# Five of the seven small steps of the row scales of x's second half move from VectorE to GpSimd

## The chip, the cores and the metric

The kernel runs on one core of a Trainium2 chip. Such a core has five engines that each work through their own queue of instructions in order: TensorE (PE; its weight loads are listed as PEld), VectorE (DVE), ScalarE (ACT), GpSimd (POOL) and SyncE (SP), which here only issues transfers. They wait for each other by semaphores. The metric is the time of one execution on the device, in microseconds; a kernel's number is the median of its timed runs.

## The reference, cut to what matters

The reference is one layer of a decoder: it normalises its input x (1024 rows of 1024 channels), scales and shifts it with a modulation that depends on c, projects it with w_in and feeds two mixers, whose outputs are merged and projected again. Only the beginning matters here:

```python
def rms_norm(x, g):
    x32 = x.astype(jnp.float32)
    y = x32 * lax.rsqrt(jnp.mean(x32 * x32, axis=-1, keepdims=True) + RMS_EPS)
    return (y * g.astype(jnp.float32)).astype(x.dtype)
...
    mod = jax.nn.silu(c) @ w_mod + b_mod
    shift, scale, gate = jnp.split(mod, 3, axis=-1)
    h = rms_norm(x, norm_g) * (1 + scale[:, None]) + shift[:, None]
    proj = h @ w_in
```

Each row of x has one scale, 1 / sqrt(mean of squares + 1e-6).

## The kernel before

x lies in eight tiles `x_sb` of 128 rows by 1024 channels, in pairs. The function `turn(half)` takes four of these tiles. For each pair, ScalarE squares both tiles and sums each row (line 229, `junk`), so that the first two columns of a small tile `st` of 128x8 hold two sums per partition. `rstd_of` turns them into two scales in seven instructions on 128x2 values: multiply and add (L87), a square root on ScalarE (L88), a reciprocal (L89), and one Newton step on it (L93 to L96), which mends the root. Six of the seven stand on VectorE. Then VectorE multiplies both tiles of the pair by their scales (L232), 128x1024 each. TensorE turns each 128x128 block of the four tiles (L236) into banks `xt`, eight banks of 128x512 for eight blocks of 128 channels, and ScalarE or VectorE copies them out to `xT` (L238; in the second half all copies are ScalarE's). A bank can be filled only when all four tiles of the half are scaled.

Beside this runs `modulation(dt)` for each of eight blocks of channels: VectorE forms `acc` from five eighths of w_mod's block (L251, then four times L253), TensorE adds the other three eighths and `acc` in matrix products of one column (L258, L262, called products here), and VectorE makes the pair `ab` of scale and shift from it (L270, L271). ScalarE then writes h = xT * scale + shift twice (L286 rounded `h_hi`, L287 full `hf`), VectorE their difference `h_lo` (L288), and TensorE multiplies h with three blocks of w_in (L137 to L139, `qi_ps`), 18 matrix products of 128x512 for each block of channels, 144 in all. The first of these for block 0 need only the first half of the rows. The last of the 144 ends at 75.2 us, and the rest of the kernel builds on h.

Nothing of the order on the engines is written by hand here, but for a few `order` calls: the framework builds the program with a scheduler that plans with modelled times, so the order in which an engine's instructions stand follows from what the planner thinks is ready first. The queues are strict: an instruction that waits holds up all that stand behind it on its engine.

`turn(0)` handles tiles 0 to 3, `turn(1)` tiles 4 to 7. In the orders below x_sb_110 is the pair of tiles 4 and 5, x_sb_113 the pair of tiles 6 and 7; st_283 and st_297 hold their scales.

Of the kernel before, what the change touches and what calls it, by code (L numbers as in the profile page):

```python
# [14 lines left out]
OP = mybir.AluOpType  # L15
# [4 lines left out]
D = 1024  # L20
# [5 lines left out]
EPS = 1e-6  # L26
# [8 lines left out]
def tile_hybrid(ctx, tc, x, c, norm_g, w_mod, b_mod, w_in, a_re, a_im, b_re, b_im,  # L35
                c_re, c_im, d_skip, log_dt, w_glu, b_glu, w_a_o, w_b_o, w_out,
                final_g, out):
    nc = tc.nc
# [17 lines left out]
    def bank(name):  # L56
        return ps1.tile([128, 512], F32, name=name, tag="b1")
# [15 lines left out]
    def staged(name, dtype=F32, shape=(128, L)):  # L73
        return stage.tile(list(shape), dtype, name=name, tag="sg")
# [7 lines left out]
        tc.add_manual_dep(later.ins, earlier.ins.name, mybir.DependencyInfo(  # L82
            mybir.DependencyClass.NoSync, mybir.DependencyReason.DATA), reason="order")

    def rstd_of(t, n=1):
        a, b, y, r = (t[:, i * n:(i + 1) * n] for i in range(4))
        nc.vector.tensor_scalar(a, a, 1.0 / D, EPS, op0=OP.mult, op1=OP.add)  # L87
        nc.scalar.sqrt(b, a)  # L88
        nc.vector.reciprocal(y, b)  # L89
        if n == 1:  # L90
            nc.vector.scalar_tensor_tensor(b, y, a, y, op0=OP.mult, op1=OP.mult)
        else:
            nc.vector.tensor_mul(b, y, y)  # L93
            nc.vector.tensor_mul(b, b, a)
        nc.vector.tensor_scalar(b, b, -0.5, 1.5, op0=OP.mult, op1=OP.add)
        nc.vector.tensor_mul(r, y, b)  # L96
        return r
# [75 lines left out]
    with ExitStack() as st:  # L173
# [49 lines left out]
        def turn(half):  # L223

            for t2 in range(4 * half, 4 * half + 4, 2):
                stat = p0.tile([128, 8], F32, name=f"st{t2}", tag="st", bufs=4)
                for t in (t2, t2 + 1):
                    junk = p0.tile([128, D], BF, name=f"junk{t}", tag="junk", bufs=1)
                    nc.scalar.activation(junk, x_sb[t], AF.Square, accum_out=stat[:, t - t2:t - t2 + 1])
                rstd = rstd_of(stat, 2)  # L230
                for t in (t2, t2 + 1):
                    nc.vector.tensor_scalar_mul(x_sb[t], x_sb[t], rstd[:, t - t2:t - t2 + 1])  # L232
            for k in range(ND):
                ps = bank(f"xt{half}_{k}")
                for j in range(4):
                    nc.tensor.transpose(ps[:, 128 * j:128 * j + 128],  # L236
                                        x_sb[4 * half + j][:, 128 * k:128 * k + 128], ident)
                (nc.scalar.copy if k in ((0, 1, 3, 5, 7), (0, 1, 2, 3, 4, 5, 6, 7))[half] else nc.vector.tensor_copy)(  # L238
                    xT[k][:, 512 * half:512 * half + 512], ps)

        turn(0)
        h_hi, h_lo = parts(ND, "h")
        mp = bank("mod_ps")
# [29 lines left out]

        modulation(0)
        turn(1)
        modulation(1)
        qps = [[dense_bank(f"qi{m}_ps") if 2 * m + j < 3 else bank(f"qi{m}_ps") for j in range(2)]
               for m in range(3)]
        for dt in range(ND):
# [5 lines left out]
            for sl in [slice(512 * j, 512 * j + 512) for j in range(2)] if dt < 2 else [slice(0, L)]:  # L285
# [3 lines left out]
                for m in range(3):  # L289
                    a = slice(128 * m, 128 * m + 128)  # L290
                    for j in range(sl.start // 512, sl.stop // 512):
                        b = slice(512 * j, 512 * j + 512)
# [47 lines left out]
    with ExitStack() as st:  # L340
# [23 lines left out]
        for e in range(2):  # L364
            a = slice(64 * e, 64 * e + 64)
# [98 lines left out]
        for i in groups[0] + groups[1]:  # L464
            w = 128 * (i + 1)
            for h in range(8):
                for o, n in chunks(w):
# [5 lines left out]
                    r = p1.tile([128, 512], F32, name=f"r{i}_{h}_{o}", tag="r", bufs=3)  # L473
# [4 lines left out]
                    else:  # L478
                        nc.vector.scalar_tensor_tensor(dst, r[:, :n], wi_t[:, i, h:h + 1], dst,  # L479
                                                       op0=OP.mult, op1=OP.add)  # L480
# [102 lines left out]
    for m in range(4):  # L583
# [3 lines left out]
        for half in range(2):  # L587
# [62 lines left out]
            for ri in range(2):  # L650
# [11 lines left out]
                                         op0=OP.mult, op1=OP.add)  # L662
# [5 lines left out]
            for e in range(2):  # L668
                a = slice(64 * e, 64 * e + 64)
# [25 lines left out]
    t = staged("vraw")  # L695
# [27 lines left out]
    for kt in range(ND):  # L723
        t = staged(f"wg{kt}")
# [5 lines left out]
    b = staged("bgate")[0:1]  # L730
# [30 lines left out]
    def scr(name, dtype=F32, n=6):  # L761
        return sepool.tile([128, n], dtype, name=name)
# [10 lines left out]
    half = scr("half", n=STEPS + 2)  # L773
# [258 lines left out]
    for k, (m, pieces) in enumerate(steps):  # L1032
# [8 lines left out]
        t = wpool.tile([128, D], F32, name=f"wo{k}", tag="wraw")  # L1041
# [7 lines left out]
    for t in range(NT):  # L1049
        tok = slice(128 * t, 128 * t + 128)  # L1050
        xr, y = xy[:, t % 2], xy[:, 2 + t % 2]
        nc.sync.dma_start(xr, x[tok])
        stat = const.tile([128, 8], F32, name=f"fs{t}", tag="fs", bufs=2)
# [12 lines left out]
        if t < NT - 1:  # L1066
            rstd = rstd_of(stat)
            nc.vector.scalar_tensor_tensor(y, y, rstd, fg, op0=OP.mult, op1=OP.mult)
            nc.sync.dma_start(out[tok], y)
        else:  # L1070
            a, b = slice(0, 512), slice(512, 1024)
            nc.gpsimd.tensor_mul(y[:, a], y[:, a], fg[:, a])
            nc.vector.tensor_add(stat[:, 0:1], stat[:, 0:1], stat[:, 6:7])
            rstd = rstd_of(stat)
# [32 lines left out]
```

## Time and profile before

| | us |
|---|---|
| median of 3 runs | 905.14 (904.68 to 906.53) |
| the profiled execution's own time | 904.93 |
| its span, first to last instruction | 903.2 |

TensorE is busy for 95% of the span, VectorE for 73%, ScalarE for 45%, GpSimd for 15%. In the page's 40 slices (22.6 us each) TensorE's first slice stands at 4 tenths, and all others but six at 9. The clock that was granted to TensorE has two levels, 1.2 and 2.4 GHz, which the profile writes as 0.50 and 1.00; its second slice shows 7 tenths. A timeline gives each row as start, duration, engine, line, operation, tiles written <- tiles read, and in brackets how long the engine was idle before it and for whom; rows of equal instructions that follow each other are merged (x2), and an instruction's row may overlap the next one's by its last tenth of a microsecond. TensorE's products show as two rows each.

### The profile page before, as it was taken

Reading aid. Unit: us, or ns where it says so; the run is one execution under the profiler, and the core shown is the slowest. Engines: PE = TensorE matmul, PEld = TensorE weight load, DVE = VectorE, ACT = ScalarE, POOL = GpSimd, SP = SyncE. Lnnn points to the kernel's source line nnn. Section 1 sums busy time; section 2 is a strip of 40 time slices with the busy share of each in tenths; the row PEclk is TensorE's granted clock in tenths of the full one; section 3 lists DMA queues with packets and bytes.
Section 4 is the critical chain, followed back from the end, with each engine's and each line's share of the span. In section 5 each row is a group of like instructions: output and inputs, shape, how many; then the busy total and the mean of one; then the engine's idle time right before and its main releaser. Section 6 shows DMA issues by size and latency. Waiting matters only on the chain. (4 is left out here: it accounts for less than half of the span.)

```text
span 903.2 us, 12003 instructions
## 1 busy us (share of the span) xinstructions
PE 854.9 (95%) x4105; PEld 704.1 (78%) x4105; DVE 655.7 (73%) x1381; ACT 406.5 (45%) x803; POOL 138.4 (15%) x244
## 2 busy tenths in 40 slices
PE   4999999998889998999989999999999999999996
PEld 4887788876678876878868888887888888777885
DVE  5674898488999895588236776678987776856753
ACT  7552576344446443322235555448564443432311
POOL 0000100069455944000000000000000000221000
PEclk9799999999899999999999999999999999999999
DMA  9925611363443423473334232235224232644431
GB/s 330 319 66 126 154 49 46 66 178 91 122 113 124 113 78 99 124 279 94 117 107 128 88 97 73 70 106 166 68 64 135 71 94 81 216 143 143 151 129 48
DMA packets 124228, 109.86 MB, mean 122 GB/s; under 512 B 20922, under 2 KB 108034, under 8 KB 124164
## 3 DMA queue, kind: packets, MB, share of 16 engines
q1 hardware_dynamic: 96306, 77.20, 28.3%
q10 hardware_dynamic: 27858, 31.87, 12.2%
q8 instruction: 32, 0.52, 0.3%
q14 instruction: 32, 0.26, 0.1%
HBM read 76.41 MB, written 26.22 MB: 114 GB/s over the span
## 5 line engine op out<-in xcount | busy, mean ns | idle before, releaser
L78 POOL TENSOR_TENSOR wo_l<-wo,wo_h 128x1024 fp32r<-128x1024 f32 x5 | 12.2, 2444 | 451.7 <-ACT wo_h L77 423.2
L767 DVE TENSOR_SCALAR_CACHE_REDUCE cj<-score,mid 128x1024 bf16<-128x1024 f32 (+2 forms) x72 | 67.6, 939 | 14.6 <-ACT mid L790 9.1
L894 DVE CUSTOM_DVE_ANT_0 S<-l,bias 128x384 f32<-128x384 f32 (+5 forms) x96 | 52.4, 554 | 27.1 <-PE l L891 18.5
L905 ACT ACTIVATE S<-S,stt 128x128 f32<-128x128 f32 (+7 forms) x64 | 49.1, 770 | 37.3 <-DVE stt L902 37.1
L77 ACT CAST ph<-pt 128x512 fp32r<-128x512 f32 x72 | 41.3, 585 | 43.2 <-PE pt L916 38.1
L78 DVE TENSOR_TENSOR pl<-pt,ph 128x512 fp32r<-128x512 f32 x72 | 48.9, 687 | 9.2 <-ACT ph L77 8.8
L137 PE MATMUL gb_ps<-h_hi,gb_wh 128*128 128x512 f32 x128 | 52.0, 406 | 2.0 <-ACT gbs L715 2.0
L891 PE MATMUL l<-k_s,qt 128*128 128x384 f32 (+5 forms) x192 | 49.9, 347 | 3.4 <-issue 2.3
L138 PE MATMUL gb_ps<-h_lo,gb_wh 128*128 128x512 f32 x128 | 52.3, 408 | 0.0
L139 PE MATMUL gb_ps<-h_hi,gb_wl 128*128 128x512 f32 x128 | 51.7, 404 | 0.0
L138 PE MATMUL o_ps<-wo_l,m_hi 128*128 128x512 f32 (+1 forms) x136 | 51.2, 378 | 0.0
L139 PE MATMUL o_ps<-wo_h,m_lo 128*128 128x512 f32 (+1 forms) x136 | 51.0, 378 | 0.1
L137 PE MATMUL ga_ps<-h_hi,ga_wh 128*128 128x512 f32 x128 | 50.8, 397 | 0.0
L139 PE MATMUL ga_ps<-h_hi,ga_wl 128*128 128x512 f32 x128 | 50.7, 396 | 0.0
L138 PE MATMUL ga_ps<-h_lo,ga_wh 128*128 128x512 f32 x128 | 50.2, 392 | 0.0
L474 ACT ACTIVATE r<-s 128x512 f32<-128x512 f32 (+3 forms) x80 | 39.8, 525 | 22.8 <-PE s L470 16.8
L137 PE MATMUL o_ps<-wo_h,m_hi 128*128 128x512 f32 (+1 forms) x136 | 49.4, 377 | 0.1
L479 DVE SCALAR_TENSOR_TENSOR score<-r,wi_t,score 128x512 f32<-128x512 f32 (+3 forms) x70 | 42.1, 653 | 7.5 <-ACT r L474 6.6
L916 PE MATMUL pt<-ident,S 128*128 128x128 f32 x288 | 46.3, 273 | 0.4 <-DVE S L909 0.4
L916 PEld LDWEIGHTS pt<-ident,S 128*128 128x128 f32 x288 | 36.6, 140 | 11.3 <-DVE S L909 1.0
L470 PE MATMUL s<-ki_s,qi_s 128*128 128x384 f32 (+3 forms) x160 | 42.2, 356 | 1.4 <-DVE wi_t L463 0.9
L891 PEld LDWEIGHTS l<-k_s,qt 128*128 128x128 f32 x192 | 33.9, 189 | 9.7 <-issue 2.4
(402 smaller groups left out, 2402.5 us busy)
## 6 DMA issues: line engine op xcount, KB each, us to landing
wm<-in_w_mod_dram SPq DMA_DIRECT2D x16, 512.0 KB, 6.3
x_sb<-in_x_dram SPq DMA_DIRECT2D x8, 512.0 KB, 5.5
ga_w<-in_w_in_dram SPq DMA_DIRECT2D x8, 512.0 KB, 4.1
gad<-gas ACTq DMA_DIRECT2D x8, 512.0 KB, 2.6
gb_w<-in_w_in_dram SPq DMA_DIRECT2D x8, 512.0 KB, 4.4
wg<-in_w_mod_dram SPq DMA_DIRECT2D x8, 512.0 KB, 5.2
gbd<-gbs ACTq DMA_DIRECT2D x8, 512.0 KB, 3.2
qt<-qd SPq DMA_DIRECT2D x8, 512.0 KB, 3.9
```

The source lines that it names most:

```text
L77: (hi_eng or nc.scalar.copy)(hi, src)
L78: (lo_eng or nc.vector).tensor_sub(lo, src, f32(hi))
L137: paced(nc.tensor.matmul(ps, wh, rh, start=first, stop=False))
L138: paced(nc.tensor.matmul(ps, wh, rl, start=False, stop=False))
L139: mm = nc.tensor.matmul(ps, wl, rh, start=False, stop=last)
L470: mm = nc.tensor.matmul(ps[:, :n], qs[:, h, 128 * i:128 * i + 128], ks[:, e, o:o + n], start=e == 0, stop=e == 1)
L479: nc.vector.scalar_tensor_tensor(dst, r[:, :n], wi_t[:, i, h:h + 1], dst, op0=OP.mult, op1=OP.add)
L767: nc.vector.tensor_scalar(j, src, at, None, op0=op, op1=OP.add, accum_out=dst)
L891: mm = nc.tensor.matmul(ps[:, :n], qt[:, 4 * e2 + 2 * j + g], ks[:, e, o:o + n], start=e == 0, stop=e == 1)
L894: nc.vector.tensor_tensor_reduce(out=S[:, o:o + n], in0=ps[:, :n], in1=bias[i][:, o:o + n], scale=1.0, scalar=NEG, op0=OP.add, op1=OP.max, ...
L905: nc.scalar.activation(S2[j], S2[j], AF.Exp, scale=0.125, bias=nm[:, j:j + 1], accum_out=sm[:, j:j + 1])
L916: mm = nc.tensor.transpose(ps[:, 128 * j:128 * j + 128], Ss[i, g, j][:, 128 * kb:128 * kb + 128], ident)
```

## The change

`rstd_of` gets a parameter for an engine, and `turn(1)` passes GpSimd. Of the seven steps five (the first and the last four) are then issued on GpSimd; the root stays on ScalarE and the reciprocal on VectorE. The first half of the rows and the final normalisation are as before. The new lines move all later line numbers up by 10 (L232 becomes L242, L253 L263, L262 L272 and so on).

```diff
-    def rstd_of(t, n=1):
+    def rstd_of(t, n=1, eng=None):
         a, b, y, r = (t[:, i * n:(i + 1) * n] for i in range(4))
+        if eng is not None:
+
+            eng.tensor_scalar(a, a, 1.0 / D, EPS, op0=OP.mult, op1=OP.add)
+            nc.scalar.sqrt(b, a)
+            nc.vector.reciprocal(y, b)
+            eng.tensor_mul(b, y, y)
+            eng.tensor_mul(b, b, a)
+            eng.tensor_scalar(b, b, -0.5, 1.5, op0=OP.mult, op1=OP.add)
+            eng.tensor_mul(r, y, b)
+            return r
...
-                rstd = rstd_of(stat, 2)
+                rstd = rstd_of(stat, 2, nc.gpsimd if half else None)
```

The planner puts other work in another order too, on TensorE, VectorE and ScalarE; SyncE's order of transfers stays as it was. All of it lies in the first 76 us, but for two neighbours on TensorE that change places near the middle of the program.

On VectorE, before, from the reciprocal for tiles 6 and 7 to their multiplication (acc_363 and acc_415 are the sums of blocks 1 and 2 of the modulation, L253 one term of such a sum):

```order
L89 RECIPROCAL st_297<-st_297 128x2
L253 SCALAR_TENSOR_TENSOR acc_363<-wm_116,sc,acc_363 128x256
L93 TENSOR_TENSOR st_297<-st_297 128x2
L253 SCALAR_TENSOR_TENSOR acc_363<-wm_116,sc,acc_363 128x256
L94 TENSOR_TENSOR st_297<-st_297 128x2
L251 TENSOR_SCALAR acc_415<-wm_121,sc 128x256
L253 SCALAR_TENSOR_TENSOR acc_363<-wm_116,sc,acc_363 128x256
L95 TENSOR_SCALAR st_297<-st_297 128x2
L253 SCALAR_TENSOR_TENSOR acc_415<-wm_121,sc,acc_415 128x256
L96 TENSOR_TENSOR st_297<-st_297 128x2
L253 SCALAR_TENSOR_TENSOR acc_415<-wm_121,sc,acc_415 128x256
L232 TENSOR_SCALAR x_sb_113<-x_sb_113,st_297 128x1024 x2
```

On VectorE, now, from the h_lo that stands ahead of this reciprocal to the same place and a little on (L91 the reciprocal, L263 a term, L242 the multiplication):

```order
L298 TENSOR_TENSOR h_lo_253<-hf_386,h_hi_245 128x512
L91 RECIPROCAL st_297<-st_297 128x2
L263 SCALAR_TENSOR_TENSOR acc_363<-wm_116,sc,acc_363 128x256
L78 TENSOR_TENSOR wql_412<-wq_122,wqh_411 128x384
L263 SCALAR_TENSOR_TENSOR acc_363<-wm_116,sc,acc_363 128x256
L242 TENSOR_SCALAR x_sb_113<-x_sb_113,st_297 128x1024 x2
L263 SCALAR_TENSOR_TENSOR acc_363<-wm_116,sc,acc_363 128x256
L261 TENSOR_SCALAR acc_415<-wm_121,sc 128x256
L263 SCALAR_TENSOR_TENSOR acc_415<-wm_121,sc,acc_415 128x256 x2
L280 TENSOR_TENSOR ab_377<-mod_ps,cols 128x2
```

The reciprocal stood behind the split of w_in's block (L78) and stands ahead of it; between it and the multiplication of tiles 6 and 7 there were four small steps and six instructions of the sums, and there are two terms and the split.

On TensorE, before, from the last early product with h to the first turned blocks of tiles 6 and 7 (L262 and L258 are the products of the modulation, xt_0 to xt_3 the banks of the second half):

```order
L139 MATMUL qi_ps<-h_hi_245,wql_263 128x512
L262 MATMUL mod_ps<-ones,acc_363 128x1
L258 MATMUL mod_ps<-sc,wm_116 128x1 x3
L262 MATMUL mod_ps<-ones,acc_363 128x1
L236 MATMUL xt_0_311<-ident,x_sb_113 128x128
L236 MATMUL xt_1_317<-ident,x_sb_113 128x128
L236 MATMUL xt_2_323<-ident,x_sb_113 128x128
L236 MATMUL xt_3_329<-ident,x_sb_113 128x128
L236 MATMUL xt_0_311<-ident,x_sb_113 128x128
L236 MATMUL xt_1_317<-ident,x_sb_113 128x128
L236 MATMUL xt_2_323<-ident,x_sb_113 128x128
L236 MATMUL xt_3_329<-ident,x_sb_113 128x128
```

On TensorE, now, from the turned blocks of tiles 6 and 7 on (L246 turns a block, L272 and L268 are the products):

```order
L246 MATMUL xt_3_329<-ident,x_sb_113 128x128
L246 MATMUL xt_0_311<-ident,x_sb_113 128x128
L246 MATMUL xt_1_317<-ident,x_sb_113 128x128
L246 MATMUL xt_2_323<-ident,x_sb_113 128x128
L246 MATMUL xt_3_329<-ident,x_sb_113 128x128
L272 MATMUL mod_ps<-ones,acc_363 128x1
L268 MATMUL mod_ps<-sc,wm_116 128x1 x3
L272 MATMUL mod_ps<-ones,acc_363 128x1
L246 MATMUL xt_4_335<-ident,x_sb_110 128x128 x2
L246 MATMUL xt_4_335<-ident,x_sb_113 128x128 x2
L246 MATMUL xt_5_341<-ident,x_sb_110 128x128 x2
L246 MATMUL xt_5_341<-ident,x_sb_113 128x128 x2
```

The products of block 1 stood ahead of the turned blocks of tiles 6 and 7 and now stand behind them; the next banks, xt_4 and xt_5, come right after, ahead of block 2's products.

## Rows read from the trace of the kernel before

**Rows 1.** Part 1 of the page: busy us (share of the span) xinstructions.

```profile
PE 854.9 (95%) x4105; PEld 704.1 (78%) x4105; DVE 655.7 (73%) x1381; ACT 406.5 (45%) x803; POOL 138.4 (15%) x244
```

**Rows 2.** Busy time of each engine in three stretches of TensorE's granted clock.

```profile
25.77:29.18 3.41, 2.91 (x20) 2.11 (x19) 3.41 (x11) 0.00 (x0) 0.00 (x0) 1.00 1.08 320
29.18:36.01 6.83, 6.83 (x33) 6.78 (x33) 6.40 (x18) 6.65 (x11) 0.00 (x0) 0.50 1.06 315
36.01:75.24 39.23, 39.23 (x215) 33.72 (x214) 19.98 (x40) 19.99 (x24) 0.39 (x2) 1.00 0.40 110
```

**Rows 3.** Timeline of TensorE: start us, us, instruction, idle before and releaser.

```profile
26.68 0.38 PE L262 MATMUL mod_ps<-ones,acc 128*128 128x1 f32 x2
...
27.59 0.36 PE L262 MATMUL mod_ps<-ones,acc 128*128 128x1 f32 x2
28.33 1.63 PE L236 MATMUL xt<-ident,x_sb 128*128 128x128 f32 x8 [0.38 <-DVE x_sb L232]
29.75 1.28 PE L258 MATMUL mod_ps<-sc,wm 128*128 128x1 f32 x6
...
33.03 2.80 PE L236 MATMUL xt<-ident,x_sb 128*128 128x128 f32 x12
...
49.09 0.73 PE L258 MATMUL mod_ps<-sc,wm 128*128 128x1 f32 x6
...
50.80 1.63 PE L137 MATMUL qi_ps<-h_hi,wqh 128*128 128x512 f32 x6
```

**Rows 4.** Timeline of VectorE, the scales of tiles 4 and 5.

```profile
19.81 0.17 DVE L89 RECIPROCAL st<-st 128x2 f32<-128x2 f32 x1 [0.85 <-ACT st L88]
...
20.76 0.16 DVE L270 TENSOR_TENSOR ab<-mod_ps,cols 128x2 f32<-128x2 f32 x1 [0.39 <-PE mod_ps L262]
...
21.04 0.56 DVE L78 TENSOR_TENSOR wql<-wq,wqh 128x384 fp32r<-128x384 f32 x1
...
21.70 1.42 DVE L232 TENSOR_SCALAR x_sb<-x_sb,st 128x1024 f32<-128x1024 f32 x2
```

**Rows 5.** Timeline of GpSimd: two dependent copies; its first TENSOR_TENSOR.

```profile
44.01 0.45 POOL L366 COPY dt<-dt 64x16 f32<-64x16 f32 x2 [42.00 <-DMA dt<-in_log_dt_dram]
...
182.65 1.06 POOL L518 TENSOR_TENSOR bx<-b_s,crd 128x512 f32<-128x512 f32 x1
```

**Rows 6.** Timeline of all engines near 300 us, GpSimd beside VectorE.

```profile
299.32 0.20 POOL L571 TENSOR_TENSOR rv<-sn_t,wrot 128x8 f32<-128x8 f32 x1
...
299.55 0.42 DVE L670 TENSOR_TENSOR hs<-ha,hb 64x254 f32<-64x254 f32 x1
299.65 0.40 POOL L573 TENSOR_TENSOR sn_t<-ct,wrot 128x16 f32<-128x16 f32 x1
```

**Rows 7.** Timeline of VectorE, the scales of tiles 6 and 7.

```profile
23.36 0.68 DVE L288 TENSOR_TENSOR h_lo<-hf,h_hi 128x512 fp32r<-128x512 f32 x1
23.96 0.48 DVE L253 SCALAR_TENSOR_TENSOR acc<-wm,sc,acc 128x256 f32<-128x256 f32 x1
24.36 0.55 DVE L78 TENSOR_TENSOR wql<-wq,wqh 128x384 fp32r<-128x384 f32 x1
24.83 0.16 DVE L89 RECIPROCAL st<-st 128x2 f32<-128x2 f32 x1
...
27.53 1.41 DVE L232 TENSOR_SCALAR x_sb<-x_sb,st 128x1024 f32<-128x1024 f32 x2
...
29.84 0.35 DVE L251 TENSOR_SCALAR acc<-wm,sc 128x256 f32<-128x256 f32 x1
```

**Rows 8.** Timeline of ScalarE, the last root and the copies after it.

```profile
23.00 0.52 ACT L77 CAST wqh<-wq 128x384 fp32r<-128x384 f32 x1
23.40 0.22 ACT L88 ACTIVATE st<-st 128x2 f32<-128x2 f32 x1
29.36 1.56 ACT L238 COPY xT<-xt 128x512 f32<-128x512 f32 x3 [5.74 <-PE xt L236]
```

**Rows 9.** TensorE's longest wait in total from 75 us on.

```profile
PE y_ps L677 <- DVE hs L671: 7.8, 6, 1.9
```

## The prediction

> **What bounds the kernel now.** I read the page first: TensorE is busy for 95% of the span [rows 1], so the change counts only if TensorE gets through its own queue sooner. The only long stretch in which it doesn't is the start, where x's second half is scaled and turned. There I read busy time by stretches, cut where the granted clock changes [rows 2]. From 36.01 to 75.24 us TensorE is busy for 39.23 of 39.23 us at full clock (2.4 GHz): nothing is waited for, and whatever time is won before 36 us arrives at 75.24 us whole. Ahead of that lie 6.83 us in which it is also busy throughout, at a granted clock of 0.50 (1.2 GHz). The price of that level stands in TensorE's timeline [rows 3]: one block's products take from 29.75 to 33.03 us, 3.28 us, and another block's, the same sixteen rows at full clock, from 49.09 to 50.80 us, 1.71 us. So the 6.83 us hold work for about 3.4 us. What went before: from 26.68 to 27.95 us TensorE had only one block's products of one column, then it was idle for 0.38 us until VectorE had scaled a tile of the last pair, and at 29.18 us the clock fell.
>
> So the question is when this last pair (tiles 6 and 7) is scaled, and what TensorE does meanwhile.
>
> **The change on VectorE and GpSimd.** For tiles 4 and 5 [rows 4] the steps lie beside a wait: the reciprocal ends at 19.98, but between the steps VectorE stands at `ab` until 20.76 and then does the split of w_in's block, so the multiplication starts at 21.70. Without the steps it can start behind the split, at 21.04 + 0.47 = 21.51, if GpSimd's four steps are done by then. No row shows such a step on GpSimd. The nearest ones: two copies on 64x16, the second of which waits for the first, take 0.45 us together [rows 5], so about 0.25 us a step with its hand-over once the second one's start is counted; and a 128x8 TENSOR_TENSOR takes 0.20 us [rows 6]. Four steps from 20.0 are done at 21.0. Gain 0.19 us.
>
> For tiles 6 and 7 [rows 7]: the multiplication of the pair before takes 1.33 us from 21.51, then the sum's first instruction (0.26: its row of 0.35 less the overlap with the next), a term (0.40, as from 23.96 to 24.36) and h_lo (0.60, 23.36 to 23.96), and the reciprocal starts at 24.10 where it started at 24.83. Its root is ready: it stands ahead of a cast now, at 23.00 in place of 23.40 [rows 8], and waits for GpSimd's first step. Even if that step gets to memory only when VectorE's multiplications end at 22.84, the root is done by 23.4, 0.7 us early; the cast that it holds up is read by the split at about 24.6 and costs nothing.
>
> Behind the reciprocal VectorE still has two terms and the split, 0.40 + 0.47 + 0.40, and is free at 24.17 + 1.27 = 25.44. In this time GpSimd does its four steps, beside VectorE instructions that each read two tiles from SBUF. What that does shows near 300 us [rows 6]: while VectorE runs such instructions of 0.42 us one behind the other, GpSimd's small ones go from 0.20 to 0.40 us. So there are three cases for the start of the multiplication: four steps of 0.25 us from 24.30, done at 25.3, so VectorE's own 25.5; four of 0.45 us (0.40 and a hand-over), 26.1; and if GpSimd gets nothing until VectorE has run out of work, 25.44 + 4 x 0.25 = 26.45. VectorE then stands and holds up all behind it (the sums of the next blocks), so a longer starvation isn't possible. I take 26.1, from the row that it is nearest to. Before it was 27.53: 1.4 us won, 1.1 to 2.0.
>
> On this contention the Trainium skill (SBUF — State Buffer, Who interferes with whom) is stricter: of a VectorE instruction with two SBUF inputs and a GpSimd one that reads SBUF, the second to issue waits for the whole of the first. The 0.40 in place of 0.20 us agrees. By the rule alone the start would be between the second and the third case.
>
> **The change on TensorE.** The products of block 1, which filled 1.27 us of the wait for tiles 6 and 7, stand behind the turned blocks of these tiles now. So TensorE idles where it worked, and of the 1.4 us only 1.4 - 1.27 = 0.1 us are left if everything else stays: its queue from the first turned block of tile 6 on is 1.27 us longer and starts 1.4 us earlier (26.1 + 0.8 in place of 28.33).
>
> What else changes is the mix. Before, the turned blocks of tiles 6 and 7 were followed by a whole block's products, 29.75 to 33.03, then twelve turned blocks in one go. Now products and turned blocks alternate (8 blocks, products, 8 blocks, half of a block's products, 8 blocks), and right behind them, before the sums of block 3, come nine matrix products of 128x512 where there were two. In the trace the clock fell after products and idle time and came back after twelve turned blocks and the first two large products [rows 2, 3]. With the same work packed denser and earlier I expect the full clock to last through most of what were the 6.83 us: 3.4 us won if all, 1.7 if half of it stays slow. I take 2.5 us.
>
> Can the others keep up? ScalarE's copies started 1.83 us behind the first multiplication [rows 7, 8], so now at 27.9; three took 1.56 us, so four about 2.1; with h_hi behind them, put at two copies' 1.0, that is 31.0. TensorE has 1.27 us of products, 16 turned blocks (12 took 2.80 at 1.2 GHz, so 1.9 at full clock) and a block's products ahead of the first that reads it, and comes there no earlier than 26.1 + 1.8 + 1.3 + 1.9 + 1.7 = 32.8. VectorE's sum for block 3 starts at about 26.1 + 4.2 = 30.3; before it started at 29.84 without a wait, so its weights are there. Neither is late.
>
> **Sum.** 0.1 + 2.5 = 2.6 us, rounded to 2.7 for the 0.19 us won at tiles 4 and 5, of which half reaches TensorE. The profiled execution took 904.93 us, 1.7 more than its span of 903.2, and is 0.2 us off the median of 905.14: 905.14 - 2.7 = 902.4. Nothing from 75 us on has a time of its own: TensorE's longest wait there, 7.8 us in all, is for VectorE's work on the same data [rows 9], and moves along.
>
> **Rivals.**
>
> Same clock. If the clock falls near 29 us again for 6.83 us, 0.1 us is won: 905.0. For it: the products stay, and TensorE now idles about 0.5 us more before the last pair. Against it: what follows that wait is eight turned blocks, then eight more after 1.3 us.
>
> Slow steps. If a GpSimd step costs 0.7 us, more than three times the 0.20 of a 128x8 instruction, the multiplication of tiles 6 and 7 starts at 24.3 + 2.8 = 27.1, 0.4 us earlier than before, and the moved products cost 1.27: -0.9 us, which part of the clock's 3.4 us may pay: 904 to 906. For it: TENSOR_SCALAR on GpSimd has no row. Against it: a step waits at most for the instruction that it meets, and of the three none is longer than 0.55 us [rows 7].
>
> Slower: a longer stretch at 1.2 GHz. The twelve turned blocks that stood together at 33.03, ahead of the clock's return, are now spread, with products between them. If the clock falls at 29 us all the same and this no longer brings it back, it stays at 0.50 until the large products, for one more stretch like the shorter ones (3.41 us [rows 2]), half of which is lost: 905.0 + 1.7 = 906.7. It decides as soon as TensorE meets the first turned block of bank xt_4 at the low level.
>
> First use. The Trainium skill (GPSIMD Engine Reference, 2.1 Instruction dispatch) says that the first call of a freshly loaded routine costs about 6 us. A mechanism like that would sit at the first step for tiles 4 and 5, GpSimd's first arithmetic now. VectorE's reciprocal waited 0.85 us for the root there [rows 4], so about 1 us would be hidden, and any more delays the whole second half one for one; at 4 us, 3 us late, the end is near 907. The trace speaks against it: GpSimd's first TENSOR_TENSOR took 1.06 us [rows 5], as do its later ones of that size.
>
> **How the numbers follow.** My forecast has 0.62, the same clock 0.15, slow steps 0.12, the longer slow stretch 0.08, first use 0.03. A difference under 0.2% (1.8 us) can't be told from none here. Of the forecast's own range, 901.0 (everything at full clock and the multiplication at 25.5) to 903.7 (half the clock's gain), 0.06 lie within 0.2%. So faster 0.56; within 0.2% 0.06 + 0.15 + 0.12 = 0.33; slower 0.11. The range that leaves out 2 in 10 is 900.9 to 905.8.
>
> **What the profile would show.** Right: the multiplication of tiles 6 and 7 starts at 25.5 to 26.5 us, GpSimd's last four steps take 1.0 to 2.0 us between the reciprocal and it, TensorE idles 0.4 to 1 us ahead of tile 6's blocks, the granted clock stands at 1.00 for at least half of 29 to 36 us, and the last of the 144 products ends near 72.5 us. Wrong: a low clock from about 29 to 36 us or longer; a multiplication after 27; a wait of TensorE between 30 and 40 us for ScalarE's h or VectorE's sums, which I have excluded; or a time won at 75 us that is gone at the end.

## Result and profile after: 900.76 us, and where the time went

The changed kernel takes 900.76 us (median of 5 runs, 897.38 to 901.35) where the kernel before takes 905.14: a ratio of 0.9949, 95% interval 0.9930 to 0.9967. Twelve further runs of it (experiment 6) have a median of 900.41 beside 904.43, 0.9960 (0.9943 to 0.9978). The forecast was 902.4 us, 900.9 to 905.8, so the time lies just below the range: the direction was right, and 1.7 us of the gain were not foreseen (1.3 by experiment 6: 4.0 us against the 2.7 forecast). The profiled execution took 900.93 us, its span is 899.1, and TensorE is as full as before [rows 1] (busy us, share of the span, instructions):

```profile
PE 852.1 (95%) x4105; PEld 702.6 (78%) x4105; DVE 654.3 (73%) x1371; ACT 406.8 (45%) x803; POOL 140.7 (16%) x254
```

One slip of mine first. The text ahead of the result lets the last of the 144 large products end at 75.24 us. The trace of before puts it later: the last starts at 76.69, and ki_ps, the first product behind the 144, at 76.91. So "near 72.5" has to be read as 74.0 to 74.2 for these two starts. TensorE is busy without a gap up to there too, so the argument that hangs on it stands. Below I follow this ki_ps, which starts at 74.63 now: 2.28 us won there, of a span that is 4.1 us shorter.

GpSimd's timeline in the changed kernel (start us, us, instruction, idle before and its releaser):

```profile
18.20 0.19 POOL L89 TENSOR_SCALAR st<-st 128x2 f32<-128x2 f32 x1 [16.20 <-ACT junk L239]
20.01 0.20 POOL L92 TENSOR_TENSOR st<-st 128x2 f32<-128x2 f32 x1 [1.62 <-DVE st L91]
...
20.84 0.19 POOL L95 TENSOR_TENSOR st<-st 128x2 f32<-128x2 f32 x1
...
25.91 0.35 POOL L92 TENSOR_TENSOR st<-st 128x2 f32<-128x2 f32 x1 [3.97 <-DVE st L91]
26.34 0.39 POOL L93 TENSOR_TENSOR st<-st 128x2 f32<-128x2 f32 x1
26.82 0.31 POOL L94 TENSOR_SCALAR st<-st 128x2 f32<-128x2 f32 x1
27.21 0.20 POOL L95 TENSOR_TENSOR st<-st 128x2 f32<-128x2 f32 x1
```

The first step took 0.19 us, the four behind the reciprocal 0.27 to 0.29 each from start to start when VectorE stands (20.01 to 21.03), and 0.43 when it does work with two inputs (25.91 to 27.41, 1.50 us in all). VectorE and TensorE meanwhile, the rows that answer to [rows 3, 4, 7]:

```profile
22.21 0.16 DVE L280 TENSOR_TENSOR ab<-mod_ps,cols 128x2 f32<-128x2 f32 x1 [2.28 <-PE mod_ps L272]
...
22.96 1.41 DVE L242 TENSOR_SCALAR x_sb<-x_sb,st 128x1024 f32<-128x1024 f32 x2
...
25.67 0.16 DVE L91 RECIPROCAL st<-st 128x2 f32<-128x2 f32 x1
25.75 0.46 DVE L263 SCALAR_TENSOR_TENSOR acc<-wm,sc,acc 128x256 f32<-128x256 f32 x1
26.13 0.55 DVE L78 TENSOR_TENSOR wql<-wq,wqh 128x384 fp32r<-128x384 f32 x1
26.60 0.47 DVE L263 SCALAR_TENSOR_TENSOR acc<-wm,sc,acc 128x256 f32<-128x256 f32 x1
27.44 1.42 DVE L242 TENSOR_SCALAR x_sb<-x_sb,st 128x1024 f32<-128x1024 f32 x2 [0.36 <-POOL st L95]
```

```profile
18.76 1.28 PE L268 MATMUL mod_ps<-sc,wm 128*128 128x1 f32 x6
...
28.24 1.32 PE L246 MATMUL xt<-ident,x_sb 128*128 128x128 f32 x8 [0.55 <-DVE x_sb L242]
...
29.55 0.81 PE L268 MATMUL mod_ps<-sc,wm 128*128 128x1 f32 x6
...
30.44 1.07 PE L246 MATMUL xt<-ident,x_sb 128*128 128x128 f32 x8
...
74.40 0.39 PE L149 MATMUL qi_ps<-h_hi,wql 128*128 128x512 f32 x1
74.63 0.40 PE L147 MATMUL ki_ps<-h_hi,ki_wh 128*72 128x512 f32 x1
```

The multiplication of tiles 4 and 5 starts at 22.96, 1.26 us later than before, although GpSimd had its scale ready at 21.03: VectorE stands at `ab` for 2.28 us, because block 0's products run at 1.2 GHz in this execution (the first six take 1.28 us; before they took 0.79). The profile has no clock record ahead of 26.77 us here and prints 1.00; the durations tell the level. The multiplication of tiles 6 and 7 comes at 27.44, hardly earlier than before, and ScalarE, whose root was done long before [rows 8], starts its copies at 29.27 (its timeline):

```profile
24.03 0.19 ACT L90 ACTIVATE st<-st 128x2 f32<-128x2 f32 x1
...
29.27 2.05 ACT L248 COPY xT<-xt 128x512 f32<-128x512 f32 x4 [4.65 <-PE xt L246]
```

And yet 2.28 us are won, since TensorE's work behind it runs at full clock: the eight turned blocks take 1.32 us and not 1.63, the products 0.81 for six and not 1.28 to 1.42, eight more blocks 1.07. By stretches, to set against [rows 2]:

```profile
core 0: us, PE busy (x) PEld busy (x) DVE busy (x) ACT busy (x) POOL busy (x), PEclk, DMA share, GB/s
26.77:36.01 9.24, 8.68 (x63) 7.56 (x63) 8.19 (x21) 6.74 (x12) 0.50 (x2) 1.00 1.14 349
36.01:77.00 40.99, 40.99 (x221) 34.59 (x220) 25.13 (x58) 21.65 (x26) 2.25 (x29) 1.00 0.40 107
```

From 26.77 to 238.4 us the granted clock never falls. Before, 29.18 to 36.01 were at 0.50.

So where are the other 1.8 us of the span? I set the same instructions of both traces side by side. TensorE leads by 2.28 us at ki_ps, loses 1.1 at 103 us (a wait for VectorE's wi_t of 2.0 us in place of 0.9), wins most of it back by 235, and leads by 1.9 us at 455. At 475 it leads by 4.0, and so to the end. In between VectorE jumps: at L830 (L840 now) it reads a flag and skips the long search for rows that the quick selection has not settled; none of it is needed for these inputs. VectorE behind the jump, before (first fence) and after (second):

```profile
460.76 0.29 DVE L894 CUSTOM_DVE_ANT_0 S<-l,bias 128x128 f32<-128x128 f32 x1 [5.61 <-DVEq L830]
460.98 0.08 DVE L894 DVE_READ_ACCUMULATOR2_ANT stt<- 128x1 f32 x1
460.98 0.28 DVE L894 CUSTOM_DVE_ANT_0 S<-l,bias 128x128 f32<-128x128 f32 x1
463.12 0.08 DVE L894 DVE_READ_ACCUMULATOR2_ANT stt<- 128x1 f32 x1 [1.86 <-issue]
```

```profile
458.70 0.29 DVE L904 CUSTOM_DVE_ANT_0 S<-l,bias 128x128 f32<-128x128 f32 x1 [5.49 <-DVEq L840]
458.92 0.08 DVE L904 DVE_READ_ACCUMULATOR2_ANT stt<- 128x1 f32 x1
458.92 0.28 DVE L904 CUSTOM_DVE_ANT_0 S<-l,bias 128x128 f32<-128x128 f32 x1
459.13 0.08 DVE L904 DVE_READ_ACCUMULATOR2_ANT stt<- 128x1 f32 x1
```

Before, it starts at 460.76, does three instructions and then stands for 1.86 us with "issue" as the reason, that is, for nothing that the profile shows. After, there is no such wait. What TensorE waited for around it, before and after (us in total, times, longest):

```profile
PE l L891 <- DVE stt L894: 1.1, 2, 0.7
PE pt L916 <- DVE S L909: 0.4, 2, 0.2
```

```profile
PE l L901 <- DVE stt L904: 0.2, 1, 0.2
```

1.5 us against 0.2, which is not all of it. The whole can be read from the first of the products l to the first of the products pv (66 products in both, those of gb_ps among them), before and after:

```profile
455.25 0.63 PE L891 MATMUL l<-k_s,qt 128*128 128x128 f32 x4 [2.33 <-issue]
...
472.25 0.45 PE L935 MATMUL pv<-ph,v_s 128*128 128x512 f32 x1
```

```profile
453.32 0.98 PE L901 MATMUL l<-k_s,qt 128*128 128x128 f32 x4 [2.33 <-issue]
...
468.27 0.45 PE L945 MATMUL pv<-ph,v_s 128*128 128x512 f32 x1
```

17.00 us before and 14.95 now: 2.05 us. So 2.28 us in front, 0.35 lost on the way to l and 2.05 behind the jump make the 4.0 us. The DMA table of 458 to 464 us shows what runs just then, two packets of an instruction queue, about 8 KB each (the page has 32 of them, 0.26 MB), one 1.9 us behind the jump and one 2.5 us later:

```profile
q14 instruction: 2, 0.02, 0.9%
```

My reading is that code comes in pieces, and that the landing of before lies so close to the end of its piece that VectorE runs dry until the next arrives. No row says whose packets these are, so the reading needs a test. The trace has 906 instructions of VectorE up to the jump before and 897 after, those for control included: if the reading is right, the change moved the landing by nine instructions.

### The profile page after: what moved, and what is told of

The parts are those of the page before. It is cut to its first block, busy times and chain, and to the rows that moved or that the text cites. A ratio compares the mean times of both kernels' runs of the same rounds, so it can differ in the third digit from the quotient of the medians.

```text
span 899.1 us, 12003 instructions
## 1 busy us (share of the span) xinstructions
PE 852.1 (95%) x4105; PEld 702.6 (78%) x4105; DVE 654.3 (73%) x1371; ACT 406.8 (45%) x803; POOL 140.7 (16%) x254
## 5 line engine op out<-in xcount | busy, mean ns | idle before, releaser
L78 POOL TENSOR_TENSOR wo_l<-wo,wo_h 128x1024 fp32r<-128x1024 f32 x5 | 12.2, 2443 | 449.6 <-ACT wo_h L77 421.3
L78 DVE TENSOR_TENSOR pl<-pt,ph 128x512 fp32r<-128x512 f32 x72 | 48.8, 686 | 9.1 <-ACT ph L77 8.7
L484 ACT ACTIVATE r<-s 128x512 f32<-128x512 f32 (+3 forms) x80 | 39.7, 525 | 24.4 <-PE s L480 15.4
```

The source lines that it names most:

```text
L78: (lo_eng or nc.vector).tensor_sub(lo, src, f32(hi))
```

## Experiments

All were timed against the kernel before in runs on the same chip (medians of 29 to 35 runs there: 904.29 for experiments 1 to 4, 904.43 for 5 to 8, 904.81 for 9 to 12, 905.76 for 13 to 15). The executions of one kernel lie within 5 to 12 us, and the 95% intervals of the ratios reach 1.5 to 2.2 us to either side. The profiled executions are one each; there I read the multiplication of tiles 6 and 7, the start of ki_ps, the clock, and what TensorE does behind the jump.

**Does the landing cost time? Experiments 1, 2, 5, 9, 10, 13, 14.** Useless memsets on VectorE shift the landing. In 1 and 2 they are executed at the very start; in the others they stand in the search that is skipped, so nothing is executed and only the landing moves.

```
e1, e2:        for e in range(k): nc.vector.memset(useless[:, e:e + 1], 0.0)    # start; k = 9 on after, 12 on before
the others:    bits = scr("bits", I32, 31); [nc.vector.memset(bits[:, 0:1], 1) for e in range(k)]   # skipped
               # before: k = 12 (e5), 60 (e10); after: k = 9 (e9), 14 (e13), 30 (e14)
```

Expected of 1, 2 and 5:

> The changed kernel with nine useless memsets of 128x1 on VectorE right at the start, where VectorE waits for 4 us anyway. VectorE's stream ahead of the jump at L840 is then as long as before the change (906 recorded instructions, 897 without the nine). Theory 'landing': some 2.0 us of the gain have nothing to do with x; after the jump VectorE's code comes in pieces, and where the jump lands in a piece decides whether VectorE stands once more behind its fourth arithmetic instruction. Then the 1.9 us wait <-issue at L904 is back, TensorE's first L901 pairs are late by 2 us again, and the kernel takes about 902.8 us (900.8 + 2.0). Rival 'front only': all of the 4.4 us comes from the first 77 us, and the nine memsets change nothing: 900.8 us, no wait <-issue of VectorE at L904.

> The kernel before with twelve useless memsets of 128x1 on VectorE right at the start; the order of all other instructions is that of the kernel before. Theory 'landing': the jump at L830 then lands behind the end of the piece in whose last instructions it landed before, VectorE doesn't stand a second time, and the kernel takes about 903.1 us (905.1 - 2.0) although it does twelve instructions more; no wait <-issue at L894. Rival 'front only': 905.1 us, or a little more, and the 1.9 us wait stays.

> The kernel before with twelve useless memsets put into the search that VectorE jumps over at L830 (the code for rows that the quick selection did not settle): none of them is executed, and the order on every other engine and ahead of the jump is untouched. Only the place where the jump lands moves by twelve instructions. Theory 'landing': no wait <-issue at L894, the first turned block of the softmax's output (L916) comes about 6.0 us behind the jump in place of 8.1, and the kernel takes 902.4 us (904.3, the median of 35 runs of the kernel before, less 1.9). Rival 'given back': experiment 2 removed the same wait and was not faster, so the 1.9 us are lost again later or the wait is hidden: 904.3 us. Rival 'front only': the wait stays, 904.3 us.

Of 9, 10, 13 and 14:

> The changed kernel with nine useless memsets in the search that VectorE jumps over at L840; none is executed, nothing else moves. The jump lands where it lands in the kernel before. Theory 'landing reaches the end': the wait <-issue of VectorE at L904 is back with 1.6 to 2.0 us, the first L926 comes 8.0 us behind the jump in place of 6.0, and the kernel takes 902.2 us (900.4, the median of 12 runs of experiment 6, plus 1.8). Rival 'lost among the waits': the wait is back in the profile, but the median moves by less than 0.9 us, as in experiments 2 and 5: 900.4 to 901.3 us.

> The kernel before with sixty useless memsets in the search that is jumped over, none of them executed: the landing lies in the middle of a piece of code. Theory 'landing reaches the end': no wait <-issue at L894, first L916 6.0 us behind the jump, and 1.8 us less than the kernel before: 902.6 us (from 904.4, the median of 70 runs). Rival 'lost among the waits': no wait, but 903.5 to 904.4 us.

> The changed kernel with fourteen useless memsets in the search that is jumped over, none executed: the jump lands about two instructions ahead of a piece's end. If the wait behind the landing is what made experiment 9 slower: a wait <-issue of VectorE of 1.6 to 2.4 us stands behind its first or second instruction after the jump, TensorE idles 1.2 us more there than the changed kernel, and the kernel takes 901.6 to 902.8 us (900.4 plus 1.2 to 2.4). If something else made experiment 9 slow: 900.4 us, or 904 without such a wait.

> The control of experiments 9 and 13: thirty useless memsets in the search that is jumped over, none executed, so that the jump lands at the beginning of a piece. If the landing alone matters: no wait <-issue at L904 and 900.4 us, as the changed kernel. If the memsets cost by themselves: 902 us or more without such a wait.

Measured (ratio to before with its 95% interval; the wait of VectorE with reason "issue" behind the jump; TensorE's wait there for VectorE, l and pt together; TensorE's stretch from the first l to the first pv):

| kernel | median us | ratio | VectorE issue | TensorE wait | l to pv |
|---|---|---|---|---|---|
| e6 after itself | 900.41 | 0.9960 (0.9943 to 0.9978) | none | 0.3 | 15.1 |
| e14 after, 30 skipped | 900.76 | 0.9958 (0.9937 to 0.9978) | none | 0.4 | 15.2 |
| e1 after, 9 executed | 901.81 | 0.9972 (0.9949 to 0.9995) | 1.6 | 1.6 | 16.8 |
| e9 after, 9 skipped | 904.24 | 0.9991 (0.9967 to 1.0015) | 1.7 | 1.6 | 16.9 |
| e13 after, 14 skipped | 904.01 | 0.9995 (0.9979 to 1.0011) | at the first instruction | 3.2 | 17.8 |
| e2 before, 12 executed | 904.82 | 1.0003 (0.9986 to 1.0019) | none | 1.9 | 15.0 |
| e5 before, 12 skipped | 903.94 | 0.9996 (0.9976 to 1.0016) | none | 0.3 | 15.0 |
| e10 before, 60 skipped | 904.52 | 0.9991 (0.9973 to 1.0009) | none | 0 | 15.9 |

That the place of the landing decides is shown: with the landing where it was before, the wait is there in every profile (before, 1, 9, and 3 and 7 below); moved by 9, 12, 30 or 60 it is gone; two instructions ahead of where I put a piece's end (13) VectorE's first instruction comes 6.5 us behind the jump in place of 4, and TensorE stands longest. In experiment 12 below, where the landing moves by five, a wait stands at the ninth instruction, 0.20 us long. From VectorE's list of waits in experiment 9 and its timelines in 13 and 12:

```profile
DVE stt L904 <- issue: 1.7, 1, 1.7
```

```profile
461.34 0.29 DVE L904 CUSTOM_DVE_ANT_0 S<-l,bias 128x128 f32<-128x128 f32 x1 [8.36 <-issue]
```

```profile
465.03 0.29 DVE L904 CUSTOM_DVE_ANT_0 S<-l,bias 128x128 f32<-128x128 f32 x1 [0.20 <-issue]
```

For the reading of a late piece of code speaks when the wait ends. In all seven profiles that have it, the instruction behind it starts 5.8 to 6.5 us behind the jump and 1.3 to 1.6 us behind the landing of the second of the two packets, be it the first (13), the fourth (before, 1, 3, 7, 9) or the ninth (12). Since no row says whose packets these are, it stays a reading.

What it costs TensorE is in the last column: with the wait 16.8 to 17.2 us (before, 1, 3, 7, 9) and 17.8 in 13, without it 15.0 to 15.4 (the changed kernel, 2, 4, 5, 6, 8, 11, 14, 15, and 12 with its 0.20 us) and 15.9 in 10. In that stretch the clock is at 0.50 for 3.4 us, but for 6.6 in 10 and not at all in 2. So the landing is worth about 1.9 us there, as VectorE's wait was. Right behind the jump TensorE also takes l and pt in another order than before among gb_ps's products; that is not the cause, since 1 and 9 have the order of after and the wait, 5 and 10 the order of before and none.

The medians are less sure. By the ratios, the wait put back into the changed kernel costs 1.2, 2.9 and 3.3 us (1, 9 and 13 against 0.9959, the middle of 6 and 14); taken from the kernel before, it gains 0.4 and 0.8 us (5 and 10) and nothing in 2. The intervals of 13 and 14, timed side by side, don't overlap; those of 5 and 10 hold 1.9 us as well as nothing, that of 2 ends at 1.3. So the times of 2, 5 and 10 came out as their rivals said, 1 lies between its two theories, and 9 and 13 were slower than I expected. Experiment 14 shows no cost of the skipped memsets themselves.

Some of this lies elsewhere. From ki_ps to the first l, TensorE does the same 1680 products in the same order in all seventeen profiles, and takes 375.5 to 382.9 us for them: 378.3 before, 378.7 in the changed kernel, 381.0 in experiment 9, which loses 2.0 us of its lead at 100 to 110 us, where its clock stands at 0.50 for 3.4 us. So the 2.9 us of experiment 9 are not the landing's alone.

**Order or engine? Experiments 3 and 4.** In 3 all steps are on VectorE but TensorE takes block 1's products behind the turned blocks; in 4 the steps are on GpSimd but the products stand ahead, as before.

```
e3:  order(summed_last[-1], turned1[1, 3, 3])              # in summed(1), s == 0: behind the 8th turned block
e4:  for k in range(4): order(turned1[1, k, 2], summed_last[-1])   # blocks of tile 6 behind block 1's products
```

> All five steps back on VectorE as before the change, but TensorE is made to take block 1's last seven products behind the eight turned blocks of tiles 6 and 7, as in the changed kernel. Theory 'order': what is won in the first 77 us comes from the order on TensorE (turned blocks and products alternate, and the clock stays up), not from GpSimd: multiplication of tiles 6 and 7 at about 27.5 us as before, the last of the 144 large products starts at 75.0 to 75.7 us (before 76.69, after 74.40), and, with the wait <-issue at L894 as before, the kernel takes 903.5 to 904.2 us. Rival 'engine': without GpSimd the moved products only cost their 1.27 us: last of the 144 at 76.7 to 78.0, 905.1 to 906.4 us.

> The five steps on GpSimd as in the changed kernel, but TensorE is made to take all of block 1's products ahead of the first turned block of tile 6, as before the change. Theory 'order': GpSimd alone wins little in front: multiplication of tiles 6 and 7 at 26.1 to 27.4 us, the last of the 144 large products starts at 76.0 to 76.7 us (before 76.69); VectorE's stream is ten instructions shorter than before, so there is no wait <-issue at L904, and the kernel takes 902.4 to 903.1 us. Rival 'engine': the earlier multiplication arrives on TensorE whole: last of the 144 at 74.4 to 75.3, 900.8 to 901.7 us.

Experiment 3: 904.88 us, 1.0003 (0.9983 to 1.0024); multiplication at 27.59, ki_ps at 78.09. Experiment 4: 906.76, 1.0023 (1.0003 to 1.0044); multiplication at 27.31, ki_ps at 80.15. Neither half gains. For experiment 3 and then for 4, the window of the low clock and TensorE's one wait between 26 and 76 us:

```profile
29.23:36.05 6.82, 6.82 (x34) 6.72 (x33) 4.44 (x12) 6.59 (x11) 0.00 (x0) 0.50 1.07 324
```

```profile
PE xt L238 <- DVE x_sb L234: 1.8, 1, 1.8
```

```profile
30.05:40.28 10.23, 10.23 (x44) 9.45 (x44) 7.87 (x20) 9.02 (x14) 0.00 (x0) 0.50 1.12 343
```

```profile
PE mod_ps L274 <- DVE acc L265: 1.6, 1, 1.6
```

In 3 TensorE has nothing to do while it waits 1.8 us for tile 6, in 4 it waits 1.6 us for the sum of block 1, which VectorE now does behind the multiplication; each time the clock stands at 0.50 soon after, for 6.8 and 10.2 us. Theory 'order' fell in 3, where its rival's place for ki_ps held; in 4 both theories fell. The change needs both: the earlier multiplication shortens the wait which the new order leaves without work. In the first profile it is hardly earlier in time (27.44 against 27.53), but TensorE's products with h ahead of it end later, at 27.69 where they end at 26.61 in experiment 3, so that it waits 0.55 us and not 1.8.

**Which pair? Experiments 11 and 12.**

```
rstd = rstd_of(stat, 2, nc.gpsimd if t2 == 6 else None)    # e11; t2 == 4 in e12
```

> Only the steps of tiles 6 and 7 on GpSimd; those of tiles 4 and 5 are back on VectorE. TensorE takes block 1's last seven products behind the turned blocks of tile 6, as in the changed kernel. If the front's gain is made by tiles 6 and 7 (an earlier multiplication, and with it the other order on TensorE and no low clock from 29 us on): multiplication of tiles 6 and 7 at 25.9 to 26.7 us, the last of the 144 large products at 73.5 to 74.7 us (changed kernel 73.3 to 74.4, kernel before 76.7), 900.4 to 901.5 us. If both pairs are needed: 902.5 us or more.

> Only the steps of tiles 4 and 5 on GpSimd; those of tiles 6 and 7 are back on VectorE, and TensorE takes block 1's products ahead of tile 6 as in the kernel before. If the front's gain is made by tiles 6 and 7: multiplication of tiles 4 and 5 at 21.5 us (before 21.70), that of 6 and 7 at 27.3 (27.53), a low clock of 6.8 us or more from about 29 us, the last of the 144 large products at 76.5 us (76.7), and 903.5 to 904.4 us. If tiles 4 and 5 matter: 902.5 us or less.

Tiles 6 and 7 alone: 901.34 us (ten runs), 0.9953 (0.9933 to 0.9973), multiplication at 25.96, ki_ps at 73.39, and no low clock after 27.22. That is the whole gain of the front. Tiles 4 and 5 alone: 905.96 us, 1.0014 (0.9993 to 1.0035), multiplication of 6 and 7 at 26.80, ki_ps at 76.42. The low clock from 29 us that I expected did not come (it was low from 20.36 to 27.19); TensorE waited 2.1 us in all for VectorE and ScalarE between 26 and 76 us instead, in pieces of up to 0.8. So waits alone do not bring the low clock, and what exactly does stays open.

**Is it luck of the clock? Experiments 6, 7 and 8.** 6 is the changed kernel once more. 7 and 8 add useless turnings of the identity to the kernel before and to the changed one.

```
idle = [nc.tensor.transpose(idle_ps[:, 0:128], ident, ident) for e in range(24)]
order(rows_turned, idle[7])
order(idle[8], rows_turned)
```

> The changed kernel itself once more, for a second profiled execution and more times. If the gain is front (about 2.4 us) plus landing (1.9 us): 900.0 us where the kernel before takes 904.3; no wait <-issue at L904; no low clock between 27 and 77 us whatever the clock did before; the last of the 144 large products starts at 73.9 to 74.6 us. If the first five runs were lucky: 902.0 us or more.

> The kernel before with 24 useless turnings of the identity on TensorE, eight ahead of its first instruction at 5.3 us and sixteen behind it, while it waits for x anyway; the order of everything else is untouched. It is to take the chance out of the clock's first rise: with TensorE busy from 2 to 9 us the clock should be at full level (2.4 GHz) by 19 us in every execution, as in the profiled execution of the kernel before (18.94) and not as in that of the changed one (26.77). If the clock is up already when x is turned, the 22 blocks from 13.98 us take 3.0 us in place of 5.04 and the products of block 0 start 2 us earlier, but VectorE's scales of tiles 4 and 5 (21.70) then wait for ScalarE's squares, so at most 1 us arrives at the last of the 144: 903.3 to 904.3 us. If the rise is not bound to TensorE's work ahead of it: 904.3 us. A low stretch from about 29 us on is expected all the same, since what makes it (products and a wait ahead of tile 6) is untouched.

> The changed kernel with the same 24 useless turnings. With the first rise out of the way the difference to experiment 7 is the change's own: theory 'front plus landing' expects the multiplication of tiles 6 and 7 at 25.9 to 26.4 us, no low clock from 27 to 77 us, 2.5 to 3 us less than experiment 7 at the last of the 144 large products, and 4.4 to 4.9 us less in all: 898.5 to 899.9 us. Rival 'luck': the front's gain comes from the clock's phase and not from the change; then both kernels have the same low stretches, and only the 1.9 us of the landing are between them.

Experiment 6 did what the theory said, with ki_ps 0.6 us sooner than expected: 73.56, 900.41 us, and in VectorE's timeline the two multiplications:

```profile
21.33 1.42 DVE L242 TENSOR_SCALAR x_sb<-x_sb,st 128x1024 f32<-128x1024 f32 x2
...
25.81 1.42 DVE L242 TENSOR_SCALAR x_sb<-x_sb,st 128x1024 f32<-128x1024 f32 x2 [0.37 <-POOL st L95]
```

In 7 the clock was up early, but fell again at 12.17 when x was turned, so the first rise was not fixed: this aim failed, 905.95 us, 1.0022 (1.0002 to 1.0042). The comparison of 7 and 8 still speaks: low from 29.24 to 36.06 in 7 and at full level from 27.97 on in 8, ki_ps at 76.88 and 73.34 (3.5 us), 905.95 and 900.51 us (0.9953 of the kernel before, 0.9931 to 0.9974), 5.4 us apart where 4.4 to 4.9 were expected. The phase of the clock alone does not make the gain. Of the profiled executions of kernels with GpSimd's steps for tiles 6 and 7 and the new order (the changed one, 1, 6, 8, 9, 11, 13, 14, 15) none has a low stretch between 28.3 and 77 us; of those with the kernel before's front (it, 2, 5, 7, 10) all have, 6.8 us or more. The low level is not gone from the first kind, though: in 6, 8, 9, 11 and 15 it lasts 6.8 us from 20.4 to 21.4 us on. Windows of two of the first kind, experiments 9 and 14, which had been low until 27.91 and 25.14:

```profile
27.91:36.01 8.10, 8.10 (x66) 7.71 (x66) 6.99 (x19) 8.07 (x15) 0.00 (x0) 1.00 1.10 335
```

```profile
25.14:36.01 10.87, 10.29 (x78) 9.15 (x77) 9.77 (x25) 8.33 (x15) 0.50 (x2) 1.00 1.13 341
```

**A version better than both? Experiment 15.** VectorE scales tiles 4 and 5 ahead of `ab`.

```
added = []; modulation(0); turn(1); order(added[0], scaled[5])
```

> The changed kernel, with VectorE made to scale tiles 4 and 5 ahead of block 0's pair ab (L280), for which it stood 2.28 us in the profiled execution of the changed kernel while GpSimd had the scale ready at 21.03. The reciprocal of tiles 6 and 7 then stands right behind. Expected if VectorE's queue sets the front: multiplication of tiles 4 and 5 at 21.0 us whatever the clock did, that of 6 and 7 at 24.3 to 25.0 us (25.8 in experiment 6), TensorE's first turned block of tile 6 at 25.2 us, the last of the 144 large products 0.3 to 1 us earlier than 73.6, 899.4 to 900.1 us. Rival: block 0's h comes 1.3 us later, TensorE waits for it, its idle time brings back a low clock after 27 us, and the kernel takes 901 us or more.

904.31 us, 0.9988 (0.9967 to 1.0009), where the changed kernel has 0.9959. The multiplications came at 21.25 and 24.53, as wanted, but ki_ps at 73.97 and not earlier; from TensorE's timeline:

```profile
22.15 1.94 PE L248 MATMUL xt<-ident,x_sb 128*128 128x128 f32 x8 [2.10 <-DVE x_sb L244]
```

TensorE stands 2.10 us for tile 4 without block 0's and block 1's work, which it did there before, and has that work left over later. The rival had the right sign and the wrong means, since no low clock came back between 28 and 77 us. That the kernel is 2.6 us slower than the changed one by the ratios, whose intervals still overlap, is not made by ki_ps, which is late by 0.4 us against experiment 6. In its profile the time goes between ki_ps and the first l, 382.9 us in place of 378.7: it loses 2.0 us of its lead at 100 to 110 us and 2.7 at 400 to 440, where the clock is low (windows as above, the clock third from the end):

```profile
103.00:106.41 3.41, 3.41 (x8) 2.73 (x9) 3.41 (x10) 0.13 (x1) 1.74 (x3) 0.50 0.25 53
399.96:406.79 6.83, 6.23 (x15) 4.87 (x16) 5.81 (x11) 2.48 (x4) 0.00 (x0) 0.50 0.45 151
```

Experiments 9 and 12 have a low stretch there as well, at 103 and 106 us; the kernel before and the changed one have none, and one of half the length at about 400. Whether experiment 15 has them in most executions, and whether its front brings them, is open. None of the versions beats the changed kernel.

## Why the forecast was 1.6 us too high

- **GpSimd's step: right.** 0.25 us alone and 0.45 beside VectorE were forecast, 0.27 and 0.43 came. The middle of the three cases held: 1.50 us for the four steps. On the port, the Trainium skill (SBUF — State Buffer, Who interferes with whom) says that the later of the two waits for the whole of the first instruction. The trace agrees: the three steps of 0.31 to 0.39 us in place of 0.19 end at 26.26, 26.73 and 27.13, each 0.05 us or so behind the VectorE instruction that it met (26.21, 26.68, 27.07).
- **First use: no cost.** The first TENSOR_SCALAR took 0.19 us at 18.20. The 6 us that the Trainium skill (GPSIMD Engine Reference, 2.1 Instruction dispatch) names for the first call of freshly loaded code appear in no row here.
- **The multiplications: right where `ab` does not wait.** 21.51 and 26.1 were forecast. In experiment 6 they are 21.33 and 25.81, in 14 21.36 and 25.84. In the first profile they are 22.96 and 27.44, and in 13 22.84 and 27.32, because the products ahead of `ab` ran at 1.2 GHz. My reference, [rows 4], came from an execution that had just reached full clock, and I took that for a property of the kernel.
- **The clock: right.** I forecast full level for most of 29 to 36 us, at 2.5 us gained, and it was full throughout, which by the forecast's own price is 3.4. "Same clock" and "a longer stretch" did not happen.
- **TensorE's wait ahead of tile 6: right.** 0.55 us, between 0.4 and 1 (in experiment 6 there is none). Later, until 76 us, it waits for nothing: "ScalarE and VectorE not late" held.
- **What reaches 77 us: the right size, in part by luck.** 2.7 forecast, 2.28 in the first pair of profiles. Two terms of the sum were off there and nearly cancel: TensorE's turned blocks of tile 6 started 0.1 us earlier (28.24 against 28.33) and not 1.4, so that the moved products cost 1.2 us where the sum has a gain of 0.1, and the clock gave 3.4 where it has 2.5. The other executions of the same front won 2.4 to 3.9 (74.51 to 73.04 against 76.91), and against the latest ki_ps of the kernel before's front (80.0) it is more still.
- **What failed: "Nothing from 75 us on has a time of its own".** The jump has, and the sum put it at nothing. The place where it lands moves with the number of instructions ahead of it in VectorE's stream, and the change, by moving ten of them to GpSimd, took a wait of 1.86 us off VectorE and 2.05 us off TensorE's stretch behind it. 2.7 and 2.05 make 4.7; the medians say 4.4 and 4.0, and the profiles 4.0. The wait could be read ahead of the result: [rows 9] come from TensorE's list of waits, and VectorE's list has it (`DVE stt L894 <- issue: 1.9, 1, 1.9`). I looked for what waits for data and asked of no wait what it would do if the code moved.

Open is how the two parts add up in the medians. With the wait in both kernels the change is worth 2.5, 0.8 and 0.5 us (1, 9, and 13 whose wait is longer), without it in both about 3.1 (0.9959 against 5 and 10). With twelve runs a kernel the difference is not beyond chance, and the 7.4 us by which the part from ki_ps to l differs between profiles would cover it.

## What to carry to other kernels

Moving instructions off an engine also moves the code behind them. Where that engine jumps, ask what the first instructions behind the landing are and who waits for them, look for a wait with the reason "issue" there, and test with instructions that are never executed (experiments 9 and 14 differ in nothing else). And before a stretch of low clock is taken for a property of a kernel, have a second execution of the same kernel: here ki_ps started anywhere from 76.9 to 80.0 us without the change. To price a change at one place, take the same instructions on both sides of that place in both traces (l to pv here): the spans also hold what every other place does in that execution.

## What the runs showed of the hardware

Behind the jump VectorE's first arithmetic came 3.6 to 4.2 us after the compare-and-branch, and by where the landing lies alone another 1.6 to 2.0 us were lost three instructions later, 0.2 eight instructions later (experiment 12), or 2.5 at once (experiment 13). TensorE's same 66 products took 16.8 to 17.2 us with that wait at the fourth instruction and 15.0 to 15.4 without. A 128x2 step costs GpSimd 0.19 to 0.20 us, little more than VectorE's 0.16. Turning the identity 24 times brought the clock up ahead of x (ten of x's blocks took 1.43 us in place of 2.39) but did not keep it there: it was at 0.50 again from 12.17 to 19.00 us, in which TensorE worked for 5.16 of 6.83 us (TensorE's timeline and that window):

```profile
5.43 3.57 PE L208 MATMUL idle_ps<-ident 128*128 128x128 f32 x16
10.80 1.43 PE L240 MATMUL xt<-ident,x_sb 128*128 128x128 f32 x10 [1.80 <-DVE x_sb L236]
```

```profile
12.17:19.00 6.83, 5.16 (x25) 4.89 (x25) 6.23 (x17) 4.68 (x9) 0.00 (x0) 0.50 1.05 399
```
